# A hybrid decoder layer: merges' sums, splits and sigmoids queued behind attention's instructions, and the norm of x computed from whole rows in the tiles of other sums

## The chip, the cores and the metric

The kernel runs on one core of a Trainium2 chip. The metric is device time in microseconds (us). TensorE (PE) does matmuls, VectorE (DVE), ScalarE (ACT) and GpSimd (POOL) the rest; SyncE (SP) issues most transfers. Each engine takes its own instructions in a fixed order, and each waits for the data that it needs.

## The reference

One decoder layer on x of 1024 tokens by 1024 channels, float32:

```python
h = rms_norm(x, pre_mix_g)
proj = h @ w_in                       # q/k/v of A, q/k/v of B, two gates
ya = (rms_norm(diff_attention(rope(qa), rope(ka), va, lam), diff_head_g) * (1 - lam_init)) @ w_a_out
for g, (window, dil) in enumerate(((128, 1), (512, 4), (2048, 16))):
    o_g, lse_g = dilated_group(qb[:, :, g], kb[:, :, g], vb[:, :, g], window, dil)
wts = softmax(stack(lses), axis=0)    # over the three groups
yb = einsum('gbsh,gbshd->bshd', wts, stack(outs)).reshape(b, s, B_WIDTH) @ w_b_out
x = x + rms_norm((sigmoid(gate_a) * ya + sigmoid(gate_b) * yb) @ w_mix_out, post_mix_g)
u = causal_depthwise_conv(rms_norm(x, pre_ffn_g) @ w_up, conv_w, conv_b)
x = x + rms_norm((gelu(gate) * val) @ w_down, post_ffn_g)
```

A has 4 heads of differential attention, B has 4 heads in each of three dilated groups. `rms_norm` divides by the root of the mean square of a token's row.

## The kernel before

Every float32 product is three matmuls (`mm3`, L152 to L156): a value is split into a high part `hi` (a ScalarE copy to fp32r, L149) and a low part `lo` (a VectorE subtraction, `sub`, L146), and the products hi·hi, hi·lo and lo·hi are added in PSUM. So each weight and each activation costs one instruction on ScalarE and one on VectorE before TensorE can use it. What comes first in the kernel's text is traced first; a scheduler then sets each engine's order from the traced order, priorities and modelled times, and pools of tiles add waits where a tile is used again.

**The values (0 to about 185 us).** v of all heads, x times `w_v`, is computed in seven products p1 to p7 of quarter size (Strassen's scheme), for two halves of the columns, i = 0 and 1. Each product has four steps k, and a step twelve matmuls (four token blocks m by three). The steps stand in `steps_v`: numbers 0 to 11 are p1 and p2 (p2 for both i), 12 to 31 are p5, p6, p7, p4, p3 for i = 0, and 32 on the same with p1 for i = 1. The left operands are sums of halves of x, made by `sums_x` in three passes on VectorE through tiles tagged `e` and `o` (in the trace they bear the names `sin` and `cos`, as they are the same tiles), and split into `t2`, `t3`, `t4`. p1, p6, p7 and p4 share four accumulators, `acc` x3 and `o`; p2, p5 and p3 share `s` and `pt`. After step k = 3 `take_v` copies each accumulator to a tile `yv` on ScalarE (L470 scaled by `rstd` where i = 1, L472 plain where i = 0). `fetch_v` loads raw weights, `ready_v` adds and splits them.

In the same stretch `norm_x` (L384 on) loads x by half rows, ScalarE squares and sums them (L389), and VectorE computes `rstd` by `rsqrt`; `angles` and `make_sines` compute the tables of the rotations, which `make_tables` multiplies by `rstd` and stores to `tab_d`. Which step of the loop traces each of these is set by constants: `NORM_AT` (first row of the norm), `ANGLES_AT`, `SINES_AT`, `TABLES_AT`, and `STORE_AT` (stores of finished quarters). With `NORM_AT` = 18 the eighth row of x is traced at step 25. In the p5 of i = 1 the second half of x^T is loaded again and split.

**Attention (about 185 to 930 us).** The steps of A and then of B run with the projections of the next step as filling (`interleave`); `later(n, fn)` puts a job n turns ahead. For each head of B, `merge` combines the three groups: `load_stats`, `weigh` (softmax weights, small instructions), `load` (weights and the groups' outputs to the tiles `mw` and `og`, one buffer each, on POOL's queue), and `add` (on VectorE the product L1036, two sums L1037 and L1039). `add` of the first half is followed by the load of the second. Jobs 0 to 4 of a merge are put off by (0, 1, 2, 5, 9) turns. Then `branch` multiplies the results of A (`oa`, loaded and split by `load_o`) and of B (`ob`) by their output weights, with the sigmoids of the gates on ScalarE; the sigmoids wait for the end of attention through a bias `zero`.

**The feed-forward half (about 930 us to the end)** runs `w_up`, the convolution and `w_down`. `weights(FULL, ...)` (called ahead of the loop over the last column blocks) adds and splits the first weights of a Strassen-like stage.

## Time and profile before

| | us |
|---|---|
| median of 3 runs | 1729.48 (1727.81 to 1730.75) |
| the profiled execution | 1729.41 |
| its span, first to last instruction | 1727.5 |
| TensorE busy | 1693.0 |
| VectorE busy | 1344.2 |
| ScalarE busy | 889.2 |
| GpSimd busy | 100.8 |

The granted clock of TensorE is 0.995 of full speed over the span. A timeline row gives start, duration, engine, line, operation, what it writes and reads, and in brackets how long the engine had been idle before and what ended that. The 1.9 us between the span and the time of the execution lie outside the instructions.

### The profile page before, as it was taken

To read this page: it belongs to the slowest core of one execution; us is meant where nothing else is said; L and a number is where in the kernel's file an instruction comes from. 1 tells how busy PE (TensorE), PEld (TensorE's weight loads), DVE (VectorE), ACT (ScalarE), POOL (GpSimd) and SP (SyncE) were. 2 spreads that over 40 slices of the span, in tenths; PEclk is the share of its full clock that TensorE was granted. 3 is DMA by queue.
4 is the path that set the end of the run, shared out by engine and by line. 5 is a ranking of instruction groups with operands and counts; after the bars stand their busy time and mean duration, and the time that the engine had idled before them with its cause. 6 is when DMAs were issued, how large, how long until landed. Compare 5 with 4: busy or idle time off the path is not lost. (4 is left out here: it accounts for less than half of the span.)

```text
span 1727.5 us, 23075 instructions
## 1 busy us (share of the span) xinstructions
PE 1693.0 (98%) x8076; PEld 1414.2 (82%) x8076; DVE 1344.2 (78%) x2558; ACT 889.2 (51%) x1646; POOL 100.8 (6%) x164
## 2 busy tenths in 40 slices
PE   8998999999999999999999999999999999999997
PEld 7876888888888888788878888878888888878886
DVE  8884486878777766777666765899999999689977
ACT  6634474746445776467563443454444444355463
POOL 0021000000000001100112500300000000000000
PEclk9999999999999999999999999999999999999999
DMA  8585322213122213522376532122222223197624
GB/s 255 186 282 197 108 80 68 80 67 107 59 68 74 70 54 124 167 96 72 127 279 207 185 110 79 37 92 95 83 97 75 80 93 97 58 341 217 208 79 158
DMA packets 105347, 216.41 MB, mean 125 GB/s; under 512 B 12992, under 2 KB 21888, under 8 KB 105232
## 3 DMA queue, kind: packets, MB, share of 16 engines
q1 hardware_dynamic: 91600, 176.79, 31.0%
q0 software_dynamic: 8736, 29.52, 5.1%
q10 hardware_dynamic: 4896, 8.65, 1.3%
q8 instruction: 63, 1.03, 0.3%
q14 instruction: 52, 0.43, 0.1%
HBM read 167.05 MB, written 47.86 MB: 124 GB/s over the span
## 5 line engine op out<-in xcount | busy, mean ns | idle before, releaser
L154 PE MATMUL acc<-xh,whi 128*128 128x512 f32 x768 | 304.4, 396 | 0.0
L156 PE MATMUL acc<-xl,whi 128*128 128x512 f32 x768 | 304.4, 396 | 0.0
L155 PE MATMUL acc<-xh,wlo 128*128 128x512 f32 x768 | 303.9, 396 | 0.0
L149 ACT ACTIVATE whi<-raw 128x512 fp32r<-128x512 f32 x251 | 155.9, 628 | 198.3 <-PE acc L156 121.3
L146 DVE TENSOR_TENSOR wlo<-raw,whi 128x512 fp32r<-128x512 f32 x251 | 179.3, 722 | 42.5 <-ACT whi L149 41.6
L156 PEld LDWEIGHTS acc<-xl,whi 128*128 128x128 f32 x768 | 144.9, 189 | 27.2
L154 PEld LDWEIGHTS acc<-xh,whi 128*128 128x128 f32 x768 | 144.9, 189 | 27.0 <-issue 0.2
L155 PEld LDWEIGHTS acc<-xh,wlo 128*128 128x128 f32 x768 | 144.8, 189 | 27.0
L154 PE MATMUL acc<-mh,whi 128*128 128x512 f32 x400 | 155.9, 390 | 0.3 <-ACT mh L149 0.3
L155 PE MATMUL acc<-mh,wlo 128*128 128x512 f32 x400 | 155.8, 389 | 0.0
L156 PE MATMUL acc<-ml,whi 128*128 128x512 f32 x400 | 155.4, 389 | 0.0
L639 ACT ACTIVATE t<-acc 64x512 f32<-64x512 f32 (+1 forms) x160 | 94.6, 591 | 49.4 <-PE acc L156 47.4
L1386 DVE TENSOR_TENSOR u<-acc,u 128x512 f32<-128x512 f32 x133 | 90.8, 686 | 24.6 <-PE acc L156 24.5
L149 ACT ACTIVATE whi<-s 128x512 fp32r<-128x512 f32 x76 | 47.0, 628 | 106.9 <-PE acc L156 99.4
L154 PEld LDWEIGHTS acc<-mh,whi 128*128 128x128 f32 x400 | 75.1, 188 | 16.3 <-ACT mh L149 0.5
L155 PEld LDWEIGHTS acc<-mh,wlo 128*128 128x128 f32 x400 | 75.2, 188 | 15.6
L156 PEld LDWEIGHTS acc<-ml,whi 128*128 128x128 f32 x400 | 75.1, 188 | 15.6
L640 DVE TENSOR_TENSOR t<-acc,cos 128x512 f32<-128x512 f32 x64 | 44.1, 690 | 51.4 <-ACT t L639 50.4
L1509 PE MATMUL acc<-whi,wlo 128*128 128x512 f32 x220 | 77.7, 390 | 0.0
L1508 PE MATMUL acc<-whi 128*128 128x512 f32 x220 | 76.5, 390 | 0.5 <-ACT whi L149 0.5
L1510 PE MATMUL acc<-wlo,whi 128*128 128x512 f32 x220 | 73.3, 390 | 0.0
L723 DVE CUSTOM_DVE_ANT_0 s<-s,mask_a 128x512 f32<-128x512 f32 (+3 forms) x96 | 51.7, 553 | 25.4 <-PE s L721 16.8
(385 smaller groups left out, 3951.3 us busy)
## 6 DMA issues: line engine op xcount, KB each, us to landing
raw<-in_w_in SPq DMA_DIRECT2D x96, 256.0 KB, 2.8
raw<-in_w_up SPq DMA_DIRECT2D x88, 256.0 KB, 2.8
raw<-in_w_v SPq DMA_DIRECT2D x72, 256.0 KB, 4.3
raw<-c_d SPq DMA_DIRECT2D x48, 256.0 KB, 3.8
c_d<-c SPq DMA_DIRECT2D x22, 512.0 KB, 3.0
raw<-in_w_down SPq DMA_DIRECT2D x37, 256.0 KB, 3.8
v_d<-yv POOLq DMA_DIRECT2D x32, 256.0 KB, 5.0
gt_d<-gate ACTq DMA_DIRECT2D x32, 256.0 KB, 2.1
```

What stands on the lines that cost most here:

```text
L146: eng.tensor_tensor(lo, src, hi.bitcast(F32), op=ALU.subtract)
L149: nc.scalar.activation(hi, src, AF.Copy)
L154: nc.tensor.matmul(o, sh, mh, start=first, stop=False, skip_group_check=on)
L155: nc.tensor.matmul(o, sl, mh, start=False, stop=False, skip_group_check=on)
L156: nc.tensor.matmul(o, sh, ml, start=False, stop=last, skip_group_check=on)
L639: nc.scalar.activation(t1[dst], ps[src], AF.Copy)
L640: nc.vector.tensor_tensor(t2, ps, cos[:, sl], op=ALU.mult)
L723: nc.vector.tensor_tensor_reduce(out=s_sb[:, c0:c1], in0=ps, in1=mask, scale=1.0, scalar=-3.0e38, op0=ALU.add, op1=ALU.max, accum_out=mx[: ...
L1386: nc.vector.tensor_tensor(to, made(p), x, op=ALU.add)
L1508: nc.tensor.matmul(banks[m], gh[:, tk], wh, start=f == 0, stop=False)
L1509: nc.tensor.matmul(banks[m], gl[:, tk], wh, start=False, stop=False)
L1510: nc.tensor.matmul(banks[m], gh[:, tk], wl, start=False, stop=f == NH - 1)
```

## The change

1. The start: `gpre` is loaded on ScalarE's queue and not GpSimd's; all first loads of x and weights are on SP's; the first x half comes in pieces of 128 and 384 columns, the first weight in two, and the second halves of x one step later.
2. The norm of x: `norm_x` loads whole rows of 512 KB into the tiles `sin` and `cos` of the sums, in turn, and sums a row's squares in one instruction. `NORM_AT` is 11 (was 18), `ANGLES_AT` 21 (15), `SINES_AT` 29 (28), `TABLES_AT` 34 (33).
3. The copies of p7 and p4 for i = 0 are scaled by `rstd`, as those of i = 1 were, and `put_v` no longer scales these quarters. The tables are stored on GpSimd's queue. After the tables, raw weights use the tables' work tiles as well (`more_tags`), and are fetched ten steps ahead, not eight. The reloads of x^T are issued at p5 and split at p7 of i = 1.
4. `behind_marks` queues instructions behind the last attention instruction traced so far, on ScalarE (its exponentials) and VectorE (its masked maxima, later the gating products): `weigh`, `add`, `split_values`, the splits of `load_o`, the sigmoids. The jobs of the first two merges are put off by (0, 2, 3, 6, 9). The first two loads of A's results are issued at the end of the step before. The bias `zero` is gone.
5. `weights(FULL, ...)` is traced at a priority raised by 40.

The core of the diff:

```diff
-XT_BUFS, ANGLES_AT, NORM_AT, SINES_AT, TABLES_AT, STORE_AT = 6, 15, 18, 28, 33, {29: 0, 30: 3, 35: 2, 38: 1}
+XT_BUFS, NORM_AT, ANGLES_AT, SINES_AT, TABLES_AT, STORE_AT = 6, 11, 21, 29, 34, {22: 0, 24: 3, 28: 2, 32: 1}
...
-    nc.gpsimd.dma_start(gpre, a["pre_mix_g"])
+    nc.scalar.dma_start(gpre, a["pre_mix_g"])
...
-    due, clock = [], [0]
+    due, clock, marks = [], [0], {}
+
+    @contextmanager
+    def behind_marks():
+
+        with ExitStack() as stack:
+            for ins in marks.values():
+                stack.enter_context(tc.issue_after(ins))
+            yield
 
...
-    ssx = tb.tile([P, 2, 8], F32, name="ssx")
+    ssx = tb.tile([P, 8], F32, name="ssx")
 
     def norm_x(m):
 
-        for half, sl in enumerate(halves()):
-            t = load_raw(a["x"][m * P : (m + 1) * P, sl], next(tags))
-            nc.scalar.activation(t, t, AF.Square, accum_out=ssx[:, half, m : m + 1])
+        t = tb.tile([P, S], F32, tag=("sin", "cos")[m % 2], name="rows")
+        dma(t, a["x"][m * P : (m + 1) * P])
+        nc.scalar.activation(t, t, AF.Square, accum_out=ssx[:, m : m + 1])
         if m == 7:
-            tt(ssx[:, 0], ssx[:, 0], ssx[:, 1], ALU.add)
-            nc.vector.tensor_copy(rstd, rsqrt(ssx[:, 0], D, tb, "rx"))
+            nc.vector.tensor_copy(rstd, rsqrt(ssx, D, tb, "rx"))
...
         for t, to in zip((tab[1], tab[0], neg), tab_d):
-            dma(to, t)
+            nc.gpsimd.dma_start(to, t)
...
-        tags = itertools.cycle(("raw", "t1", "t2"))
+        tags = rt_tags = itertools.cycle(("raw", "t1", "t2"))
+
+        def more_tags():
+
+            for tag in itertools.cycle(("ang", "kk", "sin", "cos")):
+                t = tb.tile([P, S], F32, tag=tag, name="raw")
+                for sl in halves():
+                    yield t[:, sl]
+                    yield next(rt_tags)
...
             def copy(to, r):
-                if i:
+                if i or p in ("p7", "p4"):
                     nc.scalar.activation(to, ps, AF.Copy, scale=r)
                 else:
...
             if p == "p7":
                 for m in range(4):
                     r, y = rstd[:, 4 + m : 5 + m], quarter[3, i][m]
-                    if i:
-                        plus(y, banks[False][m], r, y, ALU.add)
-                    else:
-                        tt(y, banks[False][m], y, ALU.add)
+                    plus(y, banks[False][m], r, y, ALU.add)
...
-                load_x(j, 0, *((1,) if j else (2, nc.scalar)))
+                parts = (512,) if j else (128, 384)
+                load_x(j, 0, parts)
+                if j > 1:
+                    load_x(j - 2, 1)
+                if j == 0:
+                    ready_v(j, 256)
+                c = 0
+                for w in parts:
+                    split_x(K_FIRST[j], slice(c, c + w), xts[j][:, c : c + w])
+                    c += w
                 if j:
-                    load_x(j - 1, 1)
-                w = 512 if j else 256
-                for c in range(0, 512, w):
-                    split_x(K_FIRST[j], slice(c, c + w), xts[j][:, c : c + w])
-                    if c == 0:
-                        ready_v(j)
-                if j % 2 and j > 2:
-                    sums_x(j // 2 - 1, xts[j - 2], xts[j - 3])
+                    ready_v(j)
+                if j in (4, 6):
+                    sums_x(j // 2 - 2, xts[j - 3], xts[j - 4])
+            load_x(6, 1)
             load_x(7, 1)
+            sums_x(2, xts[5], xts[4])
...
             p, i, k = steps_v[n]
-            while fetched < min(n + 8, len(steps_v)):
+            while fetched < min(n + (8 if n <= TABLES_AT else 10), len(steps_v)):
...
+            if n == TABLES_AT + 1:
+                tags = more_tags()
...
-                put_v(STORE_AT[n], 0, True)
+                put_v(STORE_AT[n], 0, STORE_AT[n] < 2)
...
             if (p, i) == ("p5", 1):
 
-                raw = load_raw(a["xT"][k][:, 512:], next(tags))
-                split_x(k, halves()[1], raw)
+                again.append(load_raw(a["xT"][k][:, 512:], next(tags)))
+            if (p, i) == ("p7", 1):
+                split_x(k, halves()[1], again[k])
...
-        for v in vs:
-            res.append(v_tiles())
-            split(*res[-1], v)
+        with behind_marks():
+            for v in vs:
+                res.append(v_tiles())
+                split(*res[-1], v)
...
-            nc.scalar.activation(sc[c][:, :w], sc[c][:, :w], AF.Exp, bias=negm[:, c : c + 1], scale=scale,
-                                 accum_out=den[:, c : c + 1])
+            exp = nc.scalar.activation(sc[c][:, :w], sc[c][:, :w], AF.Exp, bias=negm[:, c : c + 1], scale=scale,
+                                       accum_out=den[:, c : c + 1])
+        marks["ACT"] = exp.ins
...
-            nc.vector.tensor_tensor_reduce(out=s_sb[:, w], in0=ps[:, w], in1=mask, scale=1.0, scalar=-3.0e38,
-                                           op0=ALU.add, op1=ALU.max, accum_out=mx[:, j % 2 : j % 2 + 1])
+            most = nc.vector.tensor_tensor_reduce(out=s_sb[:, w], in0=ps[:, w], in1=mask, scale=1.0, scalar=-3.0e38,
+                                                  op0=ALU.add, op1=ALU.max, accum_out=mx[:, j % 2 : j % 2 + 1])
+        marks["DVE"] = most.ins
...
         def weigh():
+            with behind_marks():
+                weigh_now()
+
+        def weigh_now():
...
         def add(half):
+            with behind_marks():
+                add_now(half)
+
+        def add_now(half):
...
     def load_o(o, src, h, n, t=None):
 
-        t = t or slot("ot", dt=F32)
-        dma(t, src[h])
-        later(n, lambda: split(o[0][h], o[1][h], t))
+        if t is None:
+            t = slot("ot", dt=F32)
+        if src is not None:
+            dma(t, src[h])
+
+        def split_o():
+            with behind_marks():
+                split(o[0][h], o[1][h], t)
+
+        later(n, split_o)
+
+    ots = []
+
+    def load_ots():
+
+        for h in range(2):
+            ots.append(slot("ot", dt=F32))
+            dma(ots[h], oa_d[h])
...
-        interleave(jobs(todo), 4, (proj_b(nxt[1], nxt[2], ops_b[nxt], functools.partial(split_b, *nxt[:2]) if h % 2 else None), 8))
+        fill = proj_b(nxt[1], nxt[2], ops_b[nxt], functools.partial(split_b, *nxt[:2]) if h % 2 else None)
+        interleave(jobs(todo), 4, (itertools.chain(fill, once(load_ots)) if nxt == steps[-1] else fill, 8))
         if pair == 1 and g < 2 and h == 2:
-            for i, fn in zip((0, 1, 2, 5, 9), merge(g)):
+            for i, fn in zip((0, 2, 3, 6, 9), merge(g)):
                 later(i, fn, 0)
 
 
     pair, g, h = steps[-1]
-    ots = [slot("ot", dt=F32) for _ in range(2)]
     oa = [[slot(n) for _ in range(AH)] for n in ("oah", "oal")]
-    load_o(oa, oa_d, 0, 1, ots[0])
-    load_o(oa, oa_d, 1, 1, ots[1])
+    load_o(oa, None, 0, 1, ots[0])
+    load_o(oa, None, 1, 1, ots[1])
...
-    zero = merges.tile([P, 1], F32, name="zero")
-    nc.vector.tensor_scalar(zero, sbs[1][:, 1, 7:8], 0.0, None, op0=ALU.mult)
...
-                nc.scalar.activation(gts[d], gts[d], AF.Sigmoid, bias=zero)
+                with behind_marks():
+                    nc.scalar.activation(gts[d], gts[d], AF.Sigmoid)
...
+    for d, half, sl, ps, gt in branch(a["w_a_out"], oa, 0, gate_slot, psum, ghead):
+        marks["DVE"] = nc.vector.tensor_tensor(ya[d][:, sl], ps, gt[:, sl], op=ALU.mult).ins
...
-    ws = weights(FULL, first_ws, raw_of_a.values())
+    with tc.high_priority(offset=40):
+        ws = weights(FULL, first_ws, raw_of_a.values())
```

What this does to the engines' order is shown at three places. The rows are those of the compiled programs; the number after a name tells its copies apart. First ScalarE, around the copies of p7 for i = 0 (`yv`; those of p7 are written from `acc`, `acc`, `acc`, `o` in this order). Before, the two copies from `acc_334` and `o_335` are the last of p7's four:

```order
L472 ACTIVATE yv_474<-acc_333 128x512
L389 ACTIVATE raw_824,ssx_128<-raw_824 128x512
L395 ACT_TABLE_LOAD
L395 ACTIVATE sin_645<-sin_645 128x1024
L149 ACTIVATE whi_820<-raw_741 128x512
L389 ACTIVATE raw_803,ssx_128<-raw_803 128x512
L149 ACTIVATE whi_844<-raw_770 128x512
L389 ACTIVATE raw_827,ssx_128<-raw_827 128x512
L389 ACTIVATE raw_848,ssx_128<-raw_848 128x512
L389 ACTIVATE raw_881,ssx_128<-raw_881 128x512
L472 ACTIVATE yv_475<-acc_334 128x512
L472 ACTIVATE yv_476<-o_335 128x512
```

Now, with the copies of p7 written to `yv_476` to `yv_479`, and `edge_58` the tile that holds `rstd`:

```order
L397 ACTIVATE rows_632,ssx_128<-rows_632 128x1024
L149 ACTIVATE whi_925<-wz_135 128x512
L397 ACTIVATE rows_680,ssx_128<-rows_680 128x1024
L397 ACTIVATE rows_724,ssx_128<-rows_724 128x1024
L402 ACT_TABLE_LOAD
L402 ACTIVATE sin_816<-sin_816 128x1024
L403 ACTIVATE cos_817<-cos_817,edge_58 128x1024
L486 ACTIVATE yv_476<-acc_335,edge_58 128x512
L486 ACTIVATE yv_477<-acc_336,edge_58 128x512
L486 ACTIVATE yv_478<-acc_337,edge_58 128x512
L486 ACTIVATE yv_479<-o_338,edge_58 128x512
```

All eight Squares (`rows`, L397; five stand above this piece) and both Sin are ahead of p7's first copy, where before Squares stood between and behind its copies. The first matmul of p4, which writes `acc_335`, waits for the first of these copies.

Second VectorE, where `rstd` is computed (`rxv`, `rxy`, `rxw` are `rsqrt`'s small tiles; `kk`, `sin` and `cos` are the angles). Before:

```order
L163 TENSOR_SCALAR rxv<-ssx 128x8
L146 TENSOR_TENSOR wlo<-wz,whi 128x512
L320 TENSOR_TENSOR nlam<-ls 128x1
L166 TENSOR_SCALAR rxy<-rxv 128x8
L146 TENSOR_TENSOR wlo<-wz,whi 128x512
```

Now:

```order
L349 SCALAR_TENSOR_TENSOR sin<-kk,sin 128x1024
L163 TENSOR_SCALAR rxv<-ssx 128x8
L351 TENSOR_SCALAR sin<-sin 128x1024
L345 TENSOR_SCALAR kk<-ang 128x1024
L166 TENSOR_SCALAR rxy<-rxv 128x8
L346 TENSOR_SCALAR kk<-kk 128x1024
L174 TENSOR_TENSOR rxw<-rxy 128x8
L347 SCALAR_TENSOR_TENSOR cos<-kk,ang 128x1024
L175 TENSOR_TENSOR rxw<-rxw,rxv 128x8
L348 SCALAR_TENSOR_TENSOR cos<-kk,cos 128x1024
L176 SCALAR_TENSOR_TENSOR rxy<-rxw,rxy 128x8
L349 SCALAR_TENSOR_TENSOR cos<-kk,cos 128x1024
```

The last instructions of the angles, seven of them, now alternate with `rsqrt`'s; before they were done ahead of it.

Third VectorE in a merge of B, at the second product `mw` (`om` is the sum that frees the tile for it, `bs` and `bmx` are attention's scores and maxima, `t1`, `t2` and `kl` a rotation, `mm`, `me` and `mf` the next merge's weights). Before:

```order
L1012 TENSOR_TENSOR me_8006<-mm_8003,mr_7975 128x8 x3
L640 TENSOR_TENSOR t2_6989<-acc_6949,cos_4360 128x512
L641 TENSOR_TENSOR t1_6988<-t1_6988,sin_4361 128x512
L146 TENSOR_TENSOR wlo_7320<-raw_7325,whi_7319 128x512
L1015 TENSOR_TENSOR mf_8011<-me_8006,mr_7975 128x24
L146 TENSOR_TENSOR pt_6979<-pt_6976,pt_6979 128x256
L642 TENSOR_TENSOR t2_6989<-t2_6989,t1_6988 128x512
L1016 TENSOR_TENSOR mm_8003<-mf_8011 128x8
L1017 TENSOR_TENSOR mm_8003<-mm_8003,mf_8011 128x8
L1036 TENSOR_TENSOR mw_7674<-og_7678,mw_7674 128x1536
L1018 RECIPROCAL mm_8003<-mm_8003 128x8
L929 ISA bs_7006,bmx_7007<-s_6999,mask_b_5211 128x128
```

Now:

```order
L665 TENSOR_TENSOR t1_7975<-t1_7975,sin_4327 128x512
L954 ISA bs_7911,bmx_7912<-s_7904,mask_b_5177 128x128
L954 ISA bmx_7912 128x1
L954 ISA bs_7911,bmx_7912<-s_7904,mask_b_5177 128x256
L954 ISA bmx_7912 128x1
L1071 TENSOR_TENSOR mw_7707<-og_7711,mw_7707 128x1536
L954 ISA bs_7998,bmx_7999<-s_7991,mask_b_5177 128x128
L954 ISA bmx_7999 128x1
L954 ISA bs_7998,bmx_7999<-s_7991,mask_b_5177 128x256
L954 ISA bmx_7999 128x1
L1039 TENSOR_TENSOR mm_8012<-mr_7941 128x8
L666 TENSOR_TENSOR t2_7976<-t2_7976,t1_7975 128x512
```

The product stood 12 rows behind the `om` that frees its tile, ahead of attention's maxima; now it stands 35 rows behind, between the maxima of one part and the next, and the next merge's `mm` comes after it. Of the other two products of these merges the distances were 20 and 8 rows and are 50 and 34.

## Rows read from the trace of the kernel before

**Rows 1.** The page: busy us, share and instructions of each engine.

```profile
PE 1693.0 (98%) x8076; PEld 1414.2 (82%) x8076; DVE 1344.2 (78%) x2558; ACT 889.2 (51%) x1646; POOL 100.8 (6%) x164
```

**Rows 2.** Waits of TensorE: total us, times, longest.

```profile
PE acc L154 <- ACT yv L470: 6.8, 1, 6.8
PE s L154 <- ACT kh L831: 3.6, 2, 2.6
PE s L154 <- ACT xh L362: 3.3, 1, 3.3
PE pt L652 <- ACT bs L936: 2.1, 2, 1.1
PE s L154 <- DVE bmx L929: 1.9, 1, 1.9
...
PE s L405 <- DVE yv L320: 1.4, 1, 1.4
...
PE acc L156 <- DVE wlo L146: 0.5, 1, 0.5
```

**Rows 3.** Timeline of TensorE around p6 and p7 of i = 1.

```profile
134.57 0.39 PE L156 MATMUL o<-wlo,t2h 128*128 128x512 f32 x1
141.75 0.79 PE L154 MATMUL acc<-whi,t3h 128*128 128x512 f32 x1 [6.79 <-ACT yv L470]
...
146.53 0.40 PE L156 MATMUL acc<-wlo,t3h 128*128 128x512 f32 x1
```

**Rows 4.** Timeline of ScalarE in the same place.

```profile
138.27 0.72 ACT L362 ACTIVATE xh<-raw,edge 128x512 fp32r<-128x512 f32 x1 [3.65 <-DMA raw<-in_xT]
...
141.03 0.67 ACT L470 ACTIVATE yv<-acc,edge 128x512 f32<-128x512 f32 x1
```

**Rows 5.** Busy us of each engine from 700 to 745; granted clock third last.

```profile
700.00:745.00 45.00, 39.26 (x205) 32.48 (x204) 29.98 (x70) 20.68 (x52) 5.52 (x9) 0.96 0.55 172
```

**Rows 6.** Timeline of VectorE there: the merges' products.

```profile
703.07 1.76 DVE L1036 TENSOR_TENSOR mw<-og,mw 128x1536 f32<-128x1536 f32 x1 [4.80 <-DMA mw<-e_d]
...
738.06 1.76 DVE L1036 TENSOR_TENSOR mw<-og,mw 128x1536 f32<-128x1536 f32 x1 [5.52 <-DMA mw<-e_d]
```

**Rows 7.** Timeline of ScalarE where B's last step begins.

```profile
864.12 1.06 ACT L149 ACTIVATE oah<-ot 128x1024 fp32r<-128x1024 f32 x1 [4.03 <-DMA ot<-oa_d]
```

**Rows 8.** Timeline of TensorE: the first matmul of p4, i = 0.

```profile
76.06 0.39 PE L154 MATMUL acc<-whi,t4h 128*128 128x512 f32 x1
```

**Rows 9.** Timeline of VectorE: the last split of the sums in `t3`.

```profile
52.65 0.69 DVE L146 TENSOR_TENSOR t3l<-sin,t3h 128x512 fp32r<-128x512 f32 x1
```

**Rows 10.** Transfers: count, KB each, median us from issue to landing.

```profile
raw<-in_w_in SPq DMA_DIRECT2D x96, 256.0 KB, 2.8
...
vperm<-v_d SPq DMA_DIRECT2D x12, 512.0 KB, 4.8
...
mw<-e_d POOLq DMA_DIRECT2D x24, 256.0 KB, 6.2
...
raw<-in_x SPq DMA_DIRECT2D x16, 256.0 KB, 3.4
...
x<-in_x SPq DMA_DIRECT2D x8, 512.0 KB, 3.3
...
raw<-in_xT SPq DMA_DIRECT2D x4, 256.0 KB, 7.6
```

**Rows 11.** Timeline of ScalarE: the Square of half a row and its sum's read.

```profile
62.11 0.63 ACT L389 ACTIVATE raw<-raw 128x512 f32<-128x512 f32 x1 [3.04 <-DMA raw<-in_x]
62.65 0.19 ACT L389 ACTIVATION_READ_ACCUMULATOR raw<-raw 128x1 f32 x1
```

**Rows 12.** Groups of VectorE's instructions from 50 to 110 us: busy us, mean ns.

```profile
L339 DVE SCALAR_TENSOR_TENSOR cos<-kk,ang 128x1024 f32<-128x1024 f32 x1 | 1.2, 1219 | 0.0
...
L343 DVE TENSOR_SCALAR sin<-sin 128x1024 f32<-128x1024 f32 x1 | 0.7, 694 | 0.0
...
L176 DVE SCALAR_TENSOR_TENSOR rxy<-rxw,rxy 128x8 f32<-128x8 f32 x3 | 0.5, 165 | 0.1
```

More of the change, by code (lines that the diff above doesn't have):

```diff
@@ L3 @@
 import math
-from contextlib import ExitStack, nullcontext
+from contextlib import ExitStack, contextmanager, nullcontext
 import numpy as np
@@ L117, in load_raw @@
     def load_raw(src, tag="raw", width=512, parts=1):
-        raw = raws_in[-1].tile([P, 512], F32, tag=tag, name="raw")[:, :width]
+        raw = (raws_in[-1].tile([P, 512], F32, tag=tag, name="raw") if isinstance(tag, str) else tag)[:, :width]
         if src is None:
@@ L445, in fetch_v, with ready_v @@
                      "p4": ((1, 1),), "p3": ((0, 1),)}[p]
-            got_v[n] = [load_raw(a["w_v"][j * 4 + k][:, (2 * i + c) * 512 : (2 * i + c + 1) * 512], next(tags))
+            got_v[n] = [load_raw(a["w_v"][j * 4 + k][:, (2 * i + c) * 512 : (2 * i + c + 1) * 512], next(tags), parts=1 if n else 2)
                         for c, j in which]
-        def ready_v(n):
+        def ready_v(n, w=512):
             p, _, k = steps_v[n]
@@ L461, in ready_v @@
             ready[n] = slot_w()
-            split(*ready[n], src)
+            for c in range(0, 512, w):
+                split(*(t[:, c : c + w] for t in ready[n]), src[:, c : c + w])
         def take_v(p, i, m, ps):
@@ L532, in trunk, with load_x @@
             xts = {}
-            def load_x(j, half, parts=1, queue=nc.sync):
+            def load_x(j, half, parts=(512,)):
                 if half == 0:
                     xts[j] = prep.tile([P, S], F32, tag="xt", name="xt", bufs=XT_BUFS)
-                w = 512 // parts
-                for c in range(half * 512, half * 512 + 512, w):
-                    queue.dma_start(xts[j][:, c : c + w], a["xT"][K_FIRST[j]][:, c : c + w])
+                c = half * 512
+                for w in parts:
+                    dma(xts[j][:, c : c + w], a["xT"][K_FIRST[j]][:, c : c + w])
+                    c += w
             zeros = f32(t4[1])[:, 0]
@@ L549, in trunk @@
                 fetch_v(j)
-                load_x(j, 0, *((1,) if j else (2, nc.scalar)))
-                if j:
-                    load_x(j - 1, 1)
-                w = 512 if j else 256
-                for c in range(0, 512, w):
-                    split_x(K_FIRST[j], slice(c, c + w), xts[j][:, c : c + w])
-                    if c == 0:
-                        ready_v(j)
-                if j % 2 and j > 2:
-                    sums_x(j // 2 - 1, xts[j - 2], xts[j - 3])
+                parts = (512,) if j else (128, 384)
[5 more added lines that the diff above has]
+                c = 0
+                for w in parts:
+                    split_x(K_FIRST[j], slice(c, c + w), xts[j][:, c : c + w])
+                    c += w
+                if j:
+                    ready_v(j)
+                if j in (4, 6):
+                    sums_x(j // 2 - 2, xts[j - 3], xts[j - 4])
+            load_x(6, 1)
             load_x(7, 1)
+            sums_x(2, xts[5], xts[4])
             dma(cols, a["cols"])
@@ L573, in trunk @@
         yw = open_pool(st_y, "yw")
-        made, fetched = 12, 14
+        made, fetched, again = 12, 14, []
         quarter.update({(q, 0): new_y(f"b{q}", yw) for q in range(1, 4)})
@@ L935, in attend_b @@
             w = slice(a0, a0 + len(kb) * P)
-            nc.scalar.activation(s_sb[:, w], s_sb[:, w], AF.Exp, bias=stat[:, 0, at[j % 2] : at[j % 2] + 1], scale=scale,
-                                 accum_out=stat[:, 1, at[j % 2] : at[j % 2] + 1])
+            exp = nc.scalar.activation(s_sb[:, w], s_sb[:, w], AF.Exp, bias=stat[:, 0, at[j % 2] : at[j % 2] + 1], scale=scale,
+                                       accum_out=stat[:, 1, at[j % 2] : at[j % 2] + 1])
+        marks["ACT"] = exp.ins
         blocks = sorted(((n, b, a0 + c * P) for n, (j, kb, a0) in enumerate(spans) for c, b in enumerate(kb)),
@@ L1093, in trunk, with branch @@
     ob += [[mid_b.tile([P, S], F32R, tag=f"{n}{h}", name=n) for h in range(BH)] for n in ("obh", "obl")]
-    def branch(w_out, o, first, gate_tile, get_psum, scale=None, zero=0.0):
+    def branch(w_out, o, first, gate_tile, get_psum, scale=None):
         gts = []
@@ L1124, in gate_slot @@
         return tabs.tile([P, S], F32, tag=tag, name="gl") if tag else slot("gl", dt=F32)
-    for d, half, sl, ps, gt in branch(a["w_a_out"], oa, 0, gate_slot, psum, ghead, zero):
-        nc.vector.tensor_tensor(ya[d][:, sl], ps, gt[:, sl], op=ALU.mult)
+    for d, half, sl, ps, gt in branch(a["w_a_out"], oa, 0, gate_slot, psum, ghead):
+        marks["DVE"] = nc.vector.tensor_tensor(ya[d][:, sl], ps, gt[:, sl], op=ALU.mult).ins
         clock[0] += 1
@@ L1131, in trunk @@
     assert not due
+    marks.clear()
     st_b.close()
```

## The prediction

> **What bounds the kernel now.** First the page's busy times: TensorE is busy 1693.0 us of a span of 1727.5, 98% [rows 1]. So a change pays only where it takes away a wait of TensorE, and costs only where it adds one. Second the view of waits for TensorE: it names every releaser that ends its idle time [rows 2]. Single waits stand out: 6.8 us for a copy `yv` at L470, 3.6 us in two for `kh` at L831, 3.3 us for `xh` at the start, 2.1 us in two for `bs` at L936, 1.9 us for `bmx`, 1.4 us for `yv` at L320. The change speaks to all of these. Third, each wait on the timeline, since the engine named is only the last link.
>
> The largest: TensorE ends a matmul started at 134.57 and starts the next at 141.75. From there eleven matmuls take 4.78 us, to 146.53 [rows 3]: 0.43 us each, the pace of 1.2 GHz. After that each takes 0.227 us, the pace of 2.4 GHz, at which eleven take 2.5. Lost: 7.18 − 0.23 + 2.3 = 9.3 us. On ScalarE the copy started at 141.03, queued behind the split `xh<-raw` at 138.27, which itself idled 3.65 us for the DMA of `raw<-in_xT` [rows 4]. In the merges, VectorE idles three times at its queue's head for the loads of `mw` and `og`, 4.80 us the first time and 5.52 the last [rows 6]; behind these stand `bmx` and the rotations that TensorE needs. TensorE's waits for `kh` and `bmx` are 3.6 + 1.9 = 5.5 us; the granted clock of that stretch is 0.96, so 45 × 0.04 = 1.8 us more [rows 2, 5]. Lost: 7.3 us. Where attention ends, a split of `ot` holds ScalarE 4.03 us for its load, with the exponentials `bs` behind it [rows 7]: 2.1 us of TensorE [rows 2].
>
> **The change part by part.**
>
> *The start.* `gpre` is issued from another queue and the first `x` piece is smaller. TensorE waits 3.3 us there for `xh` [rows 2], which waits for `gpre`. Bounds: nothing, if the weights and `x` are then late, to 3.3. I take 1 us, nearer the lower end, since both are large beside `gpre`. On this a rule bears: the Trainium skill, "DMA: Bandwidth & Descriptors", section "Issuing engines are not separate DMA queues", says that transfers of all issuing engines run on the same 16 DMA engines and interleave. No row shows `gpre` alone, so this cannot be tested before the change; by the rule alone the gain would be near zero and the sum 1 us higher.
>
> *The norm of x, and the copies of p7 (a new wait).* Before, the copies of p7 and p4 at i=0 were not scaled, and TensorE went from p7 to p4 without a pause: p4 begins at 76.06 [rows 8]. Now they are scaled by `rstd`, so they wait for all eight sums of squares; and p4's first matmul reuses the accumulator that p7's first copy frees. All that TensorE does next stands behind it. The order shows eight Squares, a table load and both Sin ahead of `yv` on ScalarE.
>
> When is `rstd` there? The rows of x go through two tiles, the ones that the third sum of x used, so the first load waits for `t3l`, at 52.65 + 0.69 = 53.3 [rows 9], or 52.3 with the earlier start. The loads stand on SP in the order m 0, 2, 4, 1, 6, 3, 5, 7, each behind the Square that frees its tile. Six links follow one another: m = 0, 2, 1, 3, 5, 7 (4 and 6 run beside). A link is a load of 512 KB, 3.3 us for the same tensor in the same size [rows 10]; a Square of a whole row, by the half's row 2 × 0.53 + 0.19 = 1.25 us (the half's 0.63 less the overlap to its accumulator's read at 62.65) [rows 11]; and 0.65 us for issue and hand-over, which is my allowance. That is 5.2 us, six are 31.2: 83.5. Then VectorE: thirteen small instructions at 0.165, and between them seven of the angles, three of 1.22 and four of 0.69: 2.1 + 6.4 = 8.5 [rows 12], so 92.0. The first copy takes 0.67 (the one started at 141.03 [rows 4] let a matmul start at 141.75 [rows 3]): TensorE goes on at 92.8 instead of 76.06, **+16.7 us** with the start's gain in it. After 17 us without a matmul I charge the slow matmuls once more [rows 3]: **+2.3**.
>
> Bounds: a load of half the size takes 2.8 us and one of this size from a tensor just written 4.8 [rows 10]; six links make that 3 us less to 9 more. Below that the order excludes little: VectorE's angles, ahead of the last step, wait for the positions, whose load is now issued during p7.
>
> A page speaks against this part. The Trainium skill, "DMA: Bandwidth & Descriptors", section "Anatomy of one DMA — SWDGE (gpsimd) path", gives one transfer about 2.0 us fixed and the bytes over 436 GB/s, so an estimate of 0.6 us more for 512 KB than for 256 KB. The rows show 3.4 us for 256 KB of `in_x` in just this stretch and 3.3 for 512 KB elsewhere [rows 10], so they don't show that step; with it, from 3.4 to 4.0, the six links would be 4 us longer and the sum 1732.
>
> *What the pause gives back.* ScalarE, VectorE and the queues work on during it. The waits for `yv` at L320 (1.4) and for `wlo` by the next instruction (0.5) [rows 2] come some 30 us after p4's start, on work that will then be done: **−1.9**. The reloads of `xT` are issued earlier against TensorE, but their splits still stand ahead of p6's copies on ScalarE. The last two of these loads wait until the tables are stored. The tables' last product stands behind the 139th matmul after the pause: 95.1 + 139 × 0.227 = 126.7; a transfer of this size takes up to 4.8 us and such a reload 7.6 [rows 10], so the split comes at about 140. TensorE needs the copies 248 matmuls after the pause, at 151.4: **−9.3**. What hides it is these 11 us; if that cover goes, up to 9.3 come back.
>
> *Merges, splits of values and results, sigmoids behind attention's instructions.* On VectorE, `om` frees the buffer for the next `mw`. Between one `om` and the next product `mw` stood 12, 20 and 8 rows; now 35, 50 and 34. At 0.5 to 0.7 us for most, that is 17 us and more against a load of 6.2 [rows 10] and its issue. The three waits at VectorE's head go: **−7.3**, bounds 0 and −7.3. What is late next there: TensorE's own matmuls, since nothing else ended a wait in those 45 us. The splits of `oah` now stand behind the exponentials, and their loads are issued a step earlier: **−2.1**, bounds 0 and −2.1.
>
> *Nothing.* `weights(FULL, ...)` at higher priority: both orders read the same on ScalarE and VectorE around those splits, so what TensorE waits for there stays; likewise what waits in the feed-forward half, and the tail. The stores of the tables on POOL's queue are cheap while their readers wait for the second half of the products anyway.
>
> *Sum.* 1729.41 (the profiled execution: the span's 1727.5 and 1.9 us around it) + 16.7 + 2.3 − 1.9 − 9.3 − 7.3 − 2.1 = 1727.8; the median of the runs is 0.07 above the profiled execution: **1727.9 us**. About 0.2%, 3.5 us, is what a measurement here can tell from no change, so the forecast is: no difference that shows.
>
> **The rivals.**
>
> *`rstd` is there in time.* For it: in the code the norms are put seven steps earlier, five steps ahead of the end of p7. Against it: when `t3l` ends [rows 9], and the order. Then +16.7 and +2.3 fall away and only the start's 1 us is left: 1707.9. Half the wait gives 1718.
>
> *The loads are longer, and it is slower.* Place: the six links of `rstd`'s chain, which nothing hides. For it: they run beside the loads of `w_v`, and 4.8 us is a row for this size [rows 10]. Price 6 × 1.5 = 9 us: 1736.9. It decides from 4.1 us a load, where the sum passes 1732.9.
>
> *The merges' waits stay.* `weigh` and `add` are only queued later; if their loads are issued later too, VectorE still stands at `mw`. For it: POOL's loads wait for `om`. Against it: the rows between. Without that gain: 1735.2.
>
> **How the numbers follow.** Forecast 0.55, its own range 1720 to 1734; in time or half in time 0.20; longer loads 0.14; merges' waits stay 0.11. Faster by over 0.2% (below 1726.0): 0.20 + 0.18 of the forecast = 0.38. Within: 0.30 + 0.03 + 0.02 = 0.35. Slower: 0.07 + 0.11 + 0.09 = 0.27. With a tenth left out on either side the range is 1713 to 1737.
>
> **What would show it.** TensorE idle for some 17 us before an `acc<-whi,t4h` near 76 us, released by ScalarE's `yv` at L486, with matmuls at 0.43 us behind it; a last Square of a row at about 84 and `rxv` right behind. No wait of several us for `yv` L486 near 150; no idle time of VectorE at L1071 between 700 and 760. The forecast is wrong if the pause is under 12 or over 22 us, if the 9.3 us come back behind p6, or if TensorE waits anew between 700 and 930 us.

## The result and the profile after

The changed kernel takes 1734.74 us (median of 12 runs, 1732.4 to 1738.56), the kernel before beside it 1729.53: the ratio is 1.0027 [1.0018, 1.0035], so it is slower, by some 5 us. Forecast were 1727.9 and no difference that shows. The profiled execution took 1732.4, the fastest of the twelve, with a span of 1730.6; its 3.1 us over the span of before are what the traces can explain.

The page's busy line, then the waits of TensorE (total, times, longest), which answer to [rows 1, 2]:

```profile
PE 1689.3 (98%) x8076; PEld 1411.2 (82%) x8076; DVE 1346.7 (78%) x2549; ACT 891.3 (52%) x1631; POOL 101.7 (6%) x166
```

```profile
PE acc L154 <- ACT yv L486: 22.9, 2, 22.5
PE acc L154 <- ACT xh L370: 1.3, 1, 1.3
...
PE acc L1240 <- DVE ml L146: 1.2, 1, 1.2
PE acc L154 <- ACT yv L488: 0.9, 1, 0.9
PE acc L1241 <- DVE wlo L146: 0.7, 1, 0.7
```

The waits for `kh`, `bs`, `bmx` and the 6.8 us for `yv` are gone; one wait of 22.5 us has come (the view adds 0.4 us of another to it). TensorE's timeline there answers to [rows 8]: p4's first matmul starts at 97.82, not 76.06, and the slow matmuls behind it last to 102.53, as after the wait in [rows 3].

```profile
74.96 0.39 PE L156 MATMUL o<-wlo,t3h 128*128 128x512 f32 x1
97.82 0.80 PE L154 MATMUL acc<-whi,t4h 128*128 128x512 f32 x1 [22.48 <-ACT yv L486]
98.42 0.63 PE L155 MATMUL acc<-whi,t4l 128*128 128x512 f32 x1
...
102.53 0.40 PE L156 MATMUL acc<-wlo,t4h 128*128 128x512 f32 x1
```

What released it, back to 59 us, is in the view's chain of waits (start, duration, what):

```profile
59.10 3.29 DMA rows<-in_x
...
63.65 3.30 DMA rows<-in_x
...
68.21 5.72 DMA rows<-in_x
...
74.70 4.63 DMA raw<-in_positions
...
81.20 4.88 DMA raw<-in_w_v
...
86.10 0.69 DVE wz L328
86.80 1.15 DVE sin L348
...
93.85 1.18 DVE cos L349
...
96.87 0.18 DVE edge L399
```

The last three rows of x (m = 3, 5, 7), which the forecast had as the end of the chain, are not in it. From 74.70 on it runs over the positions' load and a load of `w_v` into VectorE's queue, where angles and `rsqrt` take turns from 86.80 to 97.05. Ahead of that the view puts the load for m = 6 (68.21), but that link is none of data. The positions' load waits for a tile that VectorE's splits from 73.99 on free, and these stand behind sums of weights, whose loads of `w_v` ended VectorE's idle time:

```profile
72.73 1.34 DVE L328 TENSOR_TENSOR wz<-raw,wz 128x512 f32<-128x512 f32 x2 [0.24 <-DMA raw<-in_w_v]
73.99 1.28 DVE L146 TENSOR_TENSOR wlo<-raw,whi 128x512 fp32r<-128x512 f32 x2
...
86.10 0.69 DVE L328 TENSOR_TENSOR wz<-raw 128x512 f32<-128x512 f32 x1 [2.34 <-DMA raw<-in_w_v]
...
89.11 0.17 DVE L163 TENSOR_SCALAR rxv<-ssx 128x8 f32<-128x8 f32 x1
```

The rows' own end, on ScalarE: the Squares for m = 5 and 7, whose loads were issued at 77.47 and 82.99. The last sum was there at 88.57, and `rxv` starts at 89.11 without a wait, since VectorE was busy until then.

```profile
81.81 1.06 ACT L397 ACTIVATE rows<-rows 128x1024 f32<-128x1024 f32 x1 [3.85 <-DMA rows<-in_x]
...
87.41 1.06 ACT L397 ACTIVATE rows<-rows 128x1024 f32<-128x1024 f32 x1 [4.45 <-DMA rows<-in_x]
88.38 0.19 ACT L397 ACTIVATION_READ_ACCUMULATOR rows<-rows 128x1 f32 x1
```

In the merges and at attention's end TensorE no longer waits (windows: busy us of PE, PEld, DVE, ACT, POOL, then the granted clock). First the kernel before:

```profile
690.00:760.00 70.00, 64.26 (x342) 53.83 (x342) 51.02 (x117) 37.56 (x85) 8.46 (x14) 0.98 0.47 144
860.00:880.00 20.00, 17.89 (x93) 14.56 (x92) 10.69 (x28) 8.85 (x23) 2.04 (x3) 1.00 0.76 273
```

Then the changed kernel:

```profile
690.00:760.00 70.00, 70.00 (x391) 60.25 (x389) 48.85 (x124) 46.34 (x102) 4.05 (x6) 1.00 0.30 95
860.00:880.00 20.00, 20.00 (x111) 17.01 (x110) 14.12 (x42) 10.63 (x25) 3.20 (x6) 1.00 0.63 205
```

By the starts of the same matmuls in both timelines:

| stretch of the program | before | after | difference | forecast |
|---|---|---|---|---|
| to p4's first matmul, i = 0 | 76.1 | 97.8 | +21.8 | +16.7 |
| to attention's projections (`acc<-xh,whi`) | 100.7 | 91.0 | −9.6 | −8.9 |
| to the first branch (`acc<-oah,whi`) | 715.4 | 703.7 | −11.7 | −9.4 |
| both branches | 88.9 | 88.9 | 0.0 | 0 |
| to the first `hn` transposed | 34.2 | 37.3 | +3.0 | 0 |
| to the end | 712.4 | 712.0 | −0.4 | 0 |

### The profile page after: what moved, and what is told of

Read it like the earlier page. It is cut to its first block, busy times and chain, and to the rows that moved or that the text cites. A ratio compares the mean times of both kernels' runs of the same rounds, so it can differ in the third digit from the quotient of the medians.

```text
span 1730.6 us, 23021 instructions
## 1 busy us (share of the span) xinstructions
PE 1689.3 (98%) x8076; PEld 1411.2 (82%) x8076; DVE 1346.7 (78%) x2549; ACT 891.3 (52%) x1631; POOL 101.7 (6%) x166
## 4 chain that ended last, share of the span: by engine, by line
PE 86%; DVE 5%; DMA 4%; issue 2%; ACT 1%; POOL 1%; SPq 0%; DVEq 0%; ACTq 0%; POOLq 0%
PE acc L154 19%; PE acc L156 19%; PE acc L155 19%; PE acc L1560 3%; PE acc L1559 3%; PE acc L1558 3%; PE o L689 2%; PE pt L676 2%; PE acc L1241 2%; PE acc L1239 2%; PE acc L1240 1%; PE o L692 1%; DVE wlo L146 1%; PE s L155 1%; PE s L156 1%
## 5 line engine op out<-in xcount | busy, mean ns | idle before, releaser
L149 ACT ACTIVATE whi<-raw 128x512 fp32r<-128x512 f32 (+1 forms) x252 | 155.8, 626 | 188.3 <-PE acc L156 111.5
L146 DVE TENSOR_TENSOR wlo<-raw,whi 128x512 fp32r<-128x512 f32 (+1 forms) x252 | 181.6, 727 | 48.4 <-ACT whi L149 45.2
```

The costliest lines, as they stand in the source:

```text
L146: eng.tensor_tensor(lo, src, hi.bitcast(F32), op=ALU.subtract)
L149: nc.scalar.activation(hi, src, AF.Copy)
```

## The experiments

"p4" is the start of p4's first matmul, i = 0; "attention" that of `acc<-xh,whi`. The sets ran on several chips, so ratios are compared.

| run | median us | ratio to before | p4 | attention | span |
|---|---|---|---|---|---|
| before | 1729.53 | | 76.1 | 176.7 | 1727.5 |
| changed | 1734.74 | 1.0027 [1.0018, 1.0035] | 97.8 | 188.9 | 1730.6 |
| e1_plain | 1721.51 | 0.9966 [0.9953, 0.9978] | 75.9 | 174.3 | 1719.6 |
| e2_four | 1727.10 | 0.9997 [0.9987, 1.0006] | 91.1 | 181.3 | 1726.5 |
| e3_plain_four | 1716.00 | 0.9928 [0.9913, 0.9943] | 77.7 | 170.8 | 1713.6 |
| e6_angles | 1720.33 | 0.9967 [0.9958, 0.9977] | 86.2 | 177.9 | 1723.2 |
| e7_half | 1731.89 | 1.0037 [1.0023, 1.0052] | 97.7 | 187.2 | 1728.0 |
| e9_behind | 1729.64 | 1.0016 [1.0005, 1.0027] | 91.8 | 181.9 | 1726.9 |
| e14_half_behind | 1722.20 | 0.9973 [0.9964, 0.9982] | 84.3 | 175.5 | 1720.1 |
| e4_nomarks | 1742.66 | 1.0081 [1.0066, 1.0096] | 99.8 | 189.7 | 1740.4 |
| e8_marks | 1721.74 | 0.9961 [0.9934, 0.9987] | 75.9 | 176.7 | 1720.1 |
| e5_sig | 1732.27 | 1.0038 [1.0023, 1.0053] | 99.1 | 189.3 | 1730.1 |
| e10_branch | 1737.37 | 1.0054 [1.0039, 1.0069] | 99.9 | 190.1 | 1737.9 |
| e11_best | 1721.24 | 0.9961 [0.9945, 0.9976] | 78.8 | 173.2 | 1722.0 |
| e12_start | 1723.45 | 0.9976 [0.9965, 0.9987] | 75.0 | 170.1 | 1723.0 |
| e13_start_marks | 1715.78 | 0.9940 [0.9926, 0.9954] | 76.5 | 171.2 | 1714.0 |

**Is it the scaled copies?** e1_plain undoes the scaling, e2_four gives the rows four tiles, e3_plain_four does both.

```diff
-                if i or p in ("p7", "p4"):
+                if i:
...
-                put_v(STORE_AT[n], 0, STORE_AT[n] < 2)
+                put_v(STORE_AT[n], 0, True)
```

> The copies of p7 and p4 for i=0 are plain again and put_v scales these quarters; the rest is the changed kernel. Theory A (the wait of p4 for rstd is the whole loss): the pause of 22.5 us and the 2.3 us of slow matmuls behind it go, of the waits of before at 87 to 107 us and at 134 us some come back (0 to 11 us, since nothing then runs ahead of TensorE): 1710 to 1721 us. Theory B (the pause only collects time that TensorE would lose later anyway, as the other engines are behind): 1727 to 1735 us, with new waits between 100 and 185 us that add up to nearly 20 us.

```diff
-        t = tb.tile([P, S], F32, tag=("sin", "cos")[m % 2], name="rows")
+        t = tb.tile([P, S], F32, tag=("sin", "cos", "ang", "kk")[m % 4], name="rows")
```

> The changed kernel, with the rows of x in four tiles in turn (sin, cos, ang, kk) and not two; copies still scaled. Theory A1 (the serial chain of row loads and Squares sets the length of the pause): two links a tile, the last Square some 12 us earlier, pause 3 to 10 us, 1715 to 1723 us. Theory A2 (the angles' instructions on VectorE and the positions' load set it): pause still 17 us or more, 1729 us or more.

> Both edits: plain copies at i=0, and rows of x in four tiles. Theory A: no pause in p7 to p4, as in the run with plain copies alone, within 3 us of it: 1709 to 1720 us. Theory B: 1727 us or more.

Without the scaling p4 starts at 75.9 and 77.7: the wait is the copies' and nothing else's. It is not the whole loss: e1_plain is 0.61% under the changed kernel, just above the range of theory A, and TensorE waits anew there (3.1 us for `whi`, 2.5 for `rstd_row`). Four tiles bring p4 forward by 6.7 us only, between the two theories (the wait falls from 22.5 to 12.7, as p7 ends later). In e2_four the last Square ends 10.6 us earlier, but the copy `edge` that makes `rstd` stands at 90.17 on VectorE. So another chain is there.

```profile
77.79 0.18 ACT L397 ACTIVATION_READ_ACCUMULATOR rows<-rows 128x1 f32 x1
```

```profile
90.17 0.16 DVE L399 COPY edge<-rxy 128x8 f32<-128x8 f32 x1
```

**Rows or VectorE?** e6_angles (on e2_four) and e9_behind (on the changed kernel) queue the angles behind `rstd`; e7_half and e14_half_behind load and square only the first half of each row, so that `rstd` is another; e14 has e9's edit too.

```diff
-            nc.vector.tensor_copy(rstd, rsqrt(ssx, D, tb, "rx"))
+            marks["rstd"] = nc.vector.tensor_copy(rstd, rsqrt(ssx, D, tb, "rx")).ins
...
-                angles(pos, *args, tb)
+                with behind_marks():
+                    angles(pos, *args, tb)
+                marks.clear()
```

> The changed kernel with the rows of x in four tiles, as in e2_four, and the angles queued on VectorE behind the copy that makes rstd. In e2_four the last row's Square ends at 77.98 and rstd is there at 90.33; in these 12.35 us VectorE runs eight instructions of the angles, one of them behind a load of the positions, among the thirteen small ones. Theory: once the rows are not late, VectorE's own order makes the pause: 13 x 0.2 us and three splits of 0.69 are 4.7 us, so p4 begins at 83 to 85 instead of 91.1, its wait is 5 to 7 us instead of 12.7, and the time 5 to 8 us under e2_four's: 1719 to 1722.5. Rival: VectorE would wait in its place for loads of w_v that stand in the same stretch: p4 not before 88, and 1725 to 1729.

> The changed kernel with the angles queued on VectorE behind the copy that makes rstd; the rows of x go through two tiles as in the changed kernel. In the changed kernel the last Square ends at 88.6 and rstd is there at 97.0; with half rows (e7_half) the Square ended 7 us earlier and rstd only 0.9, since the angles' instructions stood between. Theory: two chains end nearly together there, the rows' on ScalarE and the angles' on VectorE; with the second out of the way the first decides: 88.6 and 13 x 0.2 us, so p4 begins at 91.5 to 93 instead of 97.8, and the time is 4.5 to 6.5 us under the changed kernel's: 1728 to 1730.5. Rival: VectorE would wait for loads of w_v in the angles' place (2.15 us in e6_angles), and so would the rest: p4 at 95 or later, 1732 to 1735.

```diff
-        dma(t, a["x"][m * P : (m + 1) * P])
-        nc.scalar.activation(t, t, AF.Square, accum_out=ssx[:, m : m + 1])
+        dma(t[:, :512], a["x"][m * P : (m + 1) * P, :512])
+        nc.scalar.activation(t[:, :512], t[:, :512], AF.Square, accum_out=ssx[:, m : m + 1])
```

> The changed kernel, but each row of x is loaded and squared only over its first half (256 KB instead of 512), so rstd is not the reference's. Theory: a link of the chain is long because its load shares the DMA engines with the loads of w_v beside it (256 KB of w_v take 5.5 us there): half the bytes save 0.5 us of the Square and at most 1 us of the load in each of six links, 3 to 9 us in all; p4 begins at 89 to 95 instead of 97.8, and the time is 1726 to 1732. Rival: the load's own bytes set its time: at half of 4.65 us the six links are 17 us shorter, p4 begins at 80 to 83, and the time is 1716 to 1721.

> e9_behind with half rows as in e7_half (rstd is not the reference's). Theory: with the angles out of the way the rows' chain alone sets the pause, so the 7 us that e7_half took off that chain now show: last Square at 81 to 82, thirteen small instructions and one product of weights behind it, p4 at 84.5 to 87 instead of e9_behind's 91.8, and 1723 to 1726. Rival: VectorE's wait for a load of w_v takes their place, p4 at 88 or later: 1726.5 to 1729.5.

In e6_angles p4 starts at 86.2, between theory and rival; its ratio is 0.30% under e2_four's, some 5 us, the low end of what was expected.

VectorE's timeline in e7_half: the last row's sum starts `rxv` at 81.73 (89.11 in the changed kernel), but the eleven instructions of `rsqrt` that follow are spread between the angles, one of them behind a load of `w_v`, and `edge` comes at 95.95 (96.87). A chain 7 us shorter moved p4 by 0.1: my theory for that run had its shorter chain right and p4 wrong, and the ratio did not fall (1.0037, against 1.0027).

```profile
81.73 0.17 DVE L163 TENSOR_SCALAR rxv<-ssx 128x8 f32<-128x8 f32 x1 [0.77 <-ACT rows L397]
...
86.18 0.69 DVE L328 TENSOR_TENSOR wz<-raw 128x512 f32<-128x512 f32 x1 [1.07 <-DMA raw<-in_w_v]
86.79 1.22 DVE L348 SCALAR_TENSOR_TENSOR sin<-kk,sin 128x1024 f32<-128x1024 f32 x1
...
95.95 0.17 DVE L399 COPY edge<-rxy 128x8 f32<-128x8 f32 x1
```

In e9_behind, the same two instructions, with nothing between them but `rsqrt`:

```profile
88.44 0.17 DVE L163 TENSOR_SCALAR rxv<-ssx 128x8 f32<-128x8 f32 x1 [7.16 <-ACT rows L397]
...
90.86 0.17 DVE L399 COPY edge<-rxy 128x8 f32<-128x8 f32 x1
```

Now the rows decide, and p4 starts at 91.8. Of these 6.0 us 3.7 are left in the span and 2 in the ratio, less than the 4.5 expected at least: behind 885 TensorE waits anew, 1.6 us for `ya` and 1.4 for `mh`. With half rows as well (e14_half_behind) the last Square ends at 80.3, p4 starts at 84.3, 7.5 us earlier, and the ratio falls by 0.43%, which is 7.4 us. So there were two chains, and neither gives way alone: the rows', to 88.4 and 2.6 us of `rsqrt` (e9_behind), and VectorE's, to 96 even with the last Square at 81.7 (e7_half). The scheduler sets the order anew in each run: from the last Square to `rstd` there are 8.5 us in the changed kernel, 14.4 in e7_half, 12.4 in e2_four and 2.6 in e9_behind, by what stands between.

**What do the marks give, and where?** e4_nomarks is the changed kernel without them, e8_marks the kernel before with part 4 alone.

```diff
-            for ins in marks.values():
+            for ins in ():
```

> The changed kernel, with nothing queued behind attention's instructions (behind_marks does nothing); the merges' delays, the earlier loads of A's results and all of the first stage stay as changed. Theory A (the marks remove the waits at the merges and at the end of attention, 9.4 us): waits of TensorE between 690 and 760 and between 860 and 880 us come back, 1741 to 1745 us, the first 190 us within 2 us of the changed kernel's. Rival: the delays and earlier loads alone do it, or the later start of attention: within 2 us of 1734.7.

```diff
 (to the kernel before)
+        with behind_marks():
+            for v in vs:
...
+        def split_o():
+            with behind_marks():
+                split(o[0][h], o[1][h], t)
...
-        for i, fn in zip((0, 1, 2, 5, 9), merge(g)):
+        for i, fn in zip((0, 2, 3, 6, 9), merge(g)):
```

> The kernel before with part 4 of the change alone (merges, splits of values and results and sigmoids behind attention's instructions, the loads of the results a step earlier). Theory: what this part does is independent of the first 190 us: 11.2 us gained between 189 and 892 and 3.0 us lost behind 981, so 8.2 us under the kernel before: 1719 to 1723. Rival: the gain came from work that the pause at p4 let run ahead: then the waits of some us in the merges stay and the time is within 3 us of the kernel before.

Waits of TensorE in e4_nomarks: those of the kernel before are back [rows 2].

```profile
PE pt L676 <- ACT bs L962: 3.0, 2, 2.5
PE s L154 <- ACT kh L856: 2.7, 2, 1.4
...
PE s L154 <- DVE bmx L954: 1.4, 1, 1.4
```

The marks are worth 0.54% in the changed kernel (1.0081 to 1.0027), and all of part 4 is worth 0.39% in the kernel before: it pays without the pause, as the theory had it, and the intervals do not tell the two gains apart. Their cost is the 3.0 us behind the branches, which e4_nomarks does not have (34.2 us there) and e8_marks does (38.0). Two runs look for it.

```diff
-                with behind_marks():
-                    nc.scalar.activation(gts[d], gts[d], AF.Sigmoid)
+                nc.scalar.activation(gts[d], gts[d], AF.Sigmoid, bias=zero)
```

> The changed kernel, but its sigmoids are held back as before, by the zero bias that comes from the last step's statistics, and not queued behind attention's instructions. In the changed kernel's trace the stretch from the first matmul behind both branches (981.4) to the first transposition of hn (1018.7) is 37.3 us, in the kernel before 34.3, and with none of the marks 34.3 too. Theory: the new order of the sigmoids leaves the last products and splits of the branches late, and that is the 3.0 us: then the stretch is about 34.3 here and the time 1730 to 1733. Rival: the merges or the splits behind the marks leave something late that is paid there: then the stretch stays above 36.5 and the time within 1.5 us of 1734.7.

```diff
-        marks["DVE"] = nc.vector.tensor_tensor(ya[d][:, sl], ps, gt[:, sl], op=ALU.mult).ins
+        nc.vector.tensor_tensor(ya[d][:, sl], ps, gt[:, sl], op=ALU.mult)
```

> The changed kernel, but the first branch's products no longer mark VectorE: the sigmoids, the splits of obh and the last merge stand behind attention's last instructions only. e5_sig kept its 36.9 us from 982.1 to 1019.0, so the sigmoids are not what costs 3 us there. Theory: the last merge and the splits, held behind one product after the other in the first branch, push the rest of VectorE's work into the second branch: without it the stretch is 34.3 to 35 and the time 1731 to 1732.5. Rival: what is late there comes from the marks before the branches: then the stretch stays above 36.5, and the time within 1.5 us of the changed kernel's.

The sigmoids are not it: the stretch stays at 36.9. The first branch's marks are: without them it is 34.2. But the time is 0.27% longer, since the last merge then stands ahead of the branch's products on VectorE and takes its wait for `mw` there. VectorE's timeline in e10_branch, then TensorE's waits:

```profile
905.70 0.20 DVE L1049 RECIPROCAL mm<-mm 128x8 f32<-128x8 f32 x1
910.55 1.76 DVE L1071 TENSOR_TENSOR mw<-og,mw 128x1536 f32<-128x1536 f32 x1 [4.65 <-DMA mw<-e_d]
...
912.46 0.69 DVE L1175 TENSOR_TENSOR ya<-acc,gl 128x512 f32<-128x512 f32 x1
```

```profile
PE acc L154 <- DVE ya L1175: 7.4, 4, 3.7
```

Without these marks the branches take 97.9 us, not 88.9: the 3.0 us are the price of 9 saved, as long as the other marks stand. e11_best (e3_plain_four's edits and e10_branch's) was set down together with e10_branch and took its edit for a gain:

> The version that the runs point to: the changed kernel with plain copies of p7 and p4 at i=0, the rows of x in four tiles (both as in e3_plain_four), and the edit of e10_branch. Theory: e3_plain_four's 1716.0 less the 2 to 3 us of e10_branch: 1712.5 to 1714.5. Rival (if the marks of the first branch are not the cause): the same as e3_plain_four, 1715 to 1717.

Neither of its two cases came: it is 0.33% slower than e3_plain_four.

**What is the start worth?** e12_start is the kernel before with part 1 alone, e13_start_marks with parts 1 and 4.

```diff
 (to the kernel before)
-    nc.gpsimd.dma_start(gpre, a["pre_mix_g"])
+    nc.scalar.dma_start(gpre, a["pre_mix_g"])
...
-                load_x(j, 0, *((1,) if j else (2, nc.scalar)))
-                if j:
-                    load_x(j - 1, 1)
+                parts = (512,) if j else (128, 384)
+                load_x(j, 0, parts)
+                if j > 1:
+                    load_x(j - 2, 1)
```

> The kernel before with part 1 of the change alone: gpre from another queue, the first weights in two loads and splits, the first x in pieces of 128 and 384 columns, the loads and sums of x in the new order. In e1_plain the first real matmul began at 4.6 instead of 8.3, but two waits of 1.4 us for xh followed, and p4 began at 75.9 against 76.1 before. Theory: the start is hidden behind the loads of x that follow, so p4 begins at 75.5 to 76.1 and the time is within 1.5 us of the kernel before. Rival: the two waits belong to other parts of the change, p4 begins at 72.5 to 73.5, and the time is 2.5 to 3.5 us under the kernel before.

> The kernel before with parts 1 and 4 alone (the start, and attention's marks): the norms of x, the copies of p7 and p4, the tables' tiles and the reloads of xT are as before. Theory: the two gains lie in different stretches and add up: spans 4.5 and 7.4 us shorter make 1715.5 for the span and 1715 to 1718.5 for the time; then parts 2 and 3, the norms, scaled copies and tiles, cost the changed kernel some 15 us by themselves. Rival: they share something (the reloads of xT), and the time is 1719 or more.

p4 starts 1.1 us earlier, which is the forecast's start, yet the span is 4.5 us shorter; neither theory had that. Of the 6.8 us that TensorE waited in [rows 3] 0.5 are left, without any pause; another wait, 1.4 us before [rows 2], has grown:

```profile
PE s L405 <- DVE yv L320: 3.6, 1, 3.6
...
PE acc L154 <- ACT yv L471: 0.5, 1, 0.5
```

ScalarE's timeline of e12_start, where [rows 4] had the split at 138.27 and the copy at 141.03:

```profile
133.47 0.72 ACT L362 ACTIVATE xh<-raw,edge 128x512 fp32r<-128x512 f32 x1 [1.19 <-DMA raw<-in_xT]
...
136.33 0.67 ACT L471 ACTIVATE yv<-acc,edge 128x512 f32<-128x512 f32 x1
```

Both come some 4.7 us earlier, and with them TensorE's next product (137.06, not 141.75). The reload that the split waits for was issued 2.4 us earlier (at 128.73, not 131.10), so it also took less time; no run shows why. Parts 1 and 4 add up: 1715.78 us, ratio 0.9940, so this version beats both kernels, and e3_plain_four (0.9928) cannot be told from it. The other parts of the change then cost 1.0027 − 0.9940 = 0.87%, 15 us. The runs above say where: taking out the scaling gives 0.61% (e1_plain), four tiles for the rows another 0.38% (e3_plain_four), which is all of it within the intervals.

## Why the prediction was wrong

**The step that failed** is the pause, "rstd" at 92.0 and "+16.7" for the wait. It measured +21.8, with TensorE idle for 22.5 us. The forecast had one chain: six links of a row, then "8.5" of VectorE behind the last Square. Both numbers look near: the last Square ended at 88.6 (not 83.5), and `rstd` came 8.5 us behind it. That the second agrees is luck, as they are not one chain.

First a term was too small: the first load was issued at 53.0, and a link took 5.9 us, not 5.2. From a row's issue to its Square's start the six links took 4.7 us in the mean (3.4 to 6.8), where the sum had 3.3 for the load and 0.65 for issue and hand-over; the Square, 1.15, was a little shorter than forecast.

Second, and this decided, the path was wrong: VectorE's angles did not wait for the last Square. They were held until 86.1 by the positions' load and one of `w_v`, and e7_half shows that they hold `rstd` to 96 when the rows are there 7 us earlier. With the angles out of the way (e9_behind) `rstd` came at 91.0 although the rows were as late. The prediction had seen that the positions' load had moved into p7, and set a bound by it in words, without a price. The trace gives the price: issue at 74.7, 4.6 us for the load, 1.9 of VectorE, 4.9 for the next load of `w_v` behind it, 10.9 of VectorE, which makes 97.0.

Of the rivals "The merges' waits stay" (1735.2) is nearest in number, by accident: these waits went. The one with longer loads (1736.9, at 4.8 us a load) had half of the mechanism: the loads were longer, but e7_half halved them and the pause stayed.

**The pause's returns** (−9.3, −1.9, and +2.3 for slow matmuls) measured −9.6 in sum against −8.9: right in size. But more than half of it is not the pause's own: with the start alone (e12_start) the same stretch, from p4 to attention, takes 95.2 us and not 100.7, so 5.5 us were to be had without a pause. To count them against the pause made the change look nearly even.

**The start** (−1): right at p4 in e12_start (−1.1), where the first matmul of a product starts 3.6 us earlier and two waits for `xh` follow, 2.7 us in all; in e13_start_marks, with the same start, p4 is 0.4 later than before. What it did at 134 was not seen.

**Merges and results** (−7.3 and −2.1): in the two windows above TensorE's idle time fell by 5.7 and 2.1 us, and the clock of the first rose from 0.98 to 1.00, 70 × 0.02 = 1.4 us more; the rest of the −11.7 is spread. Right, and shown by e4_nomarks and e8_marks.

**Not foreseen:** +3.0 us behind the branches, the same marks' price (e10_branch). "What waits in the feed-forward half" stayed: the 1.3 for `wlo` is there as before.

With 5.1 − 0.7 − 2.3 + 3.0 − 0.4 the span is 4.7 us over the forecast's. What stays open: why the median lies 2.3 us above the profiled execution, and why two tiles for the rows cost 0.38% where no copy waits for `rstd` (e1_plain against e3_plain_four).

## What to carry to other kernels

Where a new wait needs a value made late, follow every queue that its makers stand in, not only the data: here instructions of other work, some behind loads of their own, stood ahead of and between those that made one small value, and held it longer than its data did; halving the data gained nothing until they were moved. Price each bound that is named in words. And try the parts of a change apart: two of them were worth 0.6%, and the others cost 0.9%.

## What the runs showed of the hardware

Loads of one size took other times by what ran beside them. Medians from 53 to 88 us (count, KB each, us from issue to landing) in e9_behind and then in e14_half_behind, whose edits differ in the rows' bytes alone; the view can tell the landing of only some of these loads (4 of 8 rows and 6 of 12 loads of `w_v`, then 3 of 8 and 6 of 14), and the medians are over those:

```profile
rows<-in_x SPq DMA_DIRECT2D x8, 512.0 KB, 4.4
raw<-in_w_v SPq DMA_DIRECT2D x12, 256.0 KB, 5.8
```

```profile
raw<-in_w_v SPq DMA_DIRECT2D x14, 256.0 KB, 3.7
rows<-in_x SPq DMA_DIRECT2D x8, 256.0 KB, 3.2
```

By these, half the bytes saved 1.2 us of the rows' loads and 2.1 of the loads of `w_v` beside them. From issue to the Square's start, which the timelines show for all eight rows, the mean fell from 4.6 to 3.4 us, by 1.2 as well. The Trainium skill, "DMA: Bandwidth & Descriptors", section "Anatomy of one DMA — SWDGE (gpsimd) path", gives a transfer 2.0 us and its bytes over 436 GB/s, by which an estimate for 256 KB less is 0.6 us. That is a fit for transfers issued by GpSimd, and these were issued by SP with others under way; the sign agrees, and the measured step is twice that. The forecast set this step aside, since its two rows did not show it.
